# Where four operations run in a four-layer fp32 kernel: row sums, reciprocals, head order and the first squares

## The chip, the cores and the metric

One core of one Trainium2 chip. The metric is the device time of one execution in microseconds (us). Three runs of the kernel before gave 2515.85, 2521.76 and 2522.85 us; their median is 2521.76 us.

## The reference

The input is 256 tokens of width 2048, in float32. Four layers follow one another, each with an rmsnorm, an input projection, a mixer, an output projection and a residual:

- **E**: 16 heads of sliding-window attention with a sink, and 8 heads of a gated recurrence.
- **O**: 16 heads of stick-breaking attention.
- **D**: for each of 16 heads three softmaxes over dilated windows (dilations 1, 4, 16), mixed by their denominators, which is one softmax over all three sets of scores; times silu(z).
- **M**: 16 heads of causal softmax attention with a linear bias (with 256 tokens there is one block only); times silu(z).

The layers D and M take shift, scale and gate from `cond @ mod_w + mod_b`, with `cond = silu(c)` a single row of 2048; the scale enters as `norm_w * (1 + scale)`. A last rmsnorm ends it. Cut to what matters:

```
mod = silu(c) @ mod_w[i] + mod_b[i]          # one row of 3 x 2048 for each of D and M
h   = rms_norm(x, norm_w[i]) * (1 + scale) + shift
p   = softmax(q k^T * scale - slope * distance)   # masked
x   = x + gate * ((p v) * silu(z)) @ w_out
```

## The kernel before, in words

Weights come from HBM as **pieces** of 128 x 1024 float32 (512 KB), through `dma_ahead` (L221) on SP's queue into 6 `raw` buffers. ScalarE rounds a piece to `whi` (`split_hi`, L233, 6 buffers), VectorE takes the rest `wlo = raw - whi` (`split_lo`, L240, 4 buffers; L255), and TensorE multiplies hi by hi, lo by hi and hi by lo (`mm_step`, L1353). A raw buffer is free again when its `wlo` is made.

All engines are issued from one program written out by hand, in order (`tc.manual_schedule`). Work beside the matmuls is kept in Python generators. After each piece `pump` (L180) advances one evacuation (`ev`, `pri`) and the first three generators of the list `bg` by one `yield` (four in the last chunk of a layer's input projection). So a `yield` is a distance of one piece in the program, and each engine carries out its own instructions strictly in that order.

- `mod_unit` (L276) adds a piece of `mod_w` times silu(c) into `macc`, 128 x 512, on VectorE, 16 steps for each of 24 columns of 512: 8 of them in layer O, 12 in D, 4 in M. `mod_fin` (L288) then sums `macc` over the partitions on GpSimd (`partition_all_reduce`, L301), adds the bias row (L303) on GpSimd, for the scale also 1 and the norm's weight (L305, L306), and stores the row to HBM from GpSimd's queue (L309). It goes to the front of `bg`.
- `head_D` (L1066, two heads for each of 8 pairs) and `head_M` (L988, four heads for each of 4 groups) keep scores with the keys on partitions. The softmax's maximum and its sum are GpSimd's `partition_all_reduce` (`amax` L977, `asum` L978); VectorE subtracts, ScalarE takes Exp, VectorE takes the reciprocal of the sum (L1004, L1087), multiplies it by half of silu2(z), and TensorE multiplies by v. The four heads of M start in the same step as far as the list's width lets them.
- silu in E and O is made of Abs, Exp, Ln and Exp on ScalarE. In D and M `silu2_gen` (L342) takes Tanh. Line L1261 loads by name the set of ScalarE's functions that holds Exp and Ln.
- `Norm.rstd` (L397) takes the power -0.5 on GpSimd, and `hq` (L404) adds the shift of half a row on GpSimd at the start of D and M.
- In `layer_DM` (L962) a pair of D takes q and k of three windows (g = 0, 1, 2) and z; z's chunk stands ahead of q and k of g = 2.
- The first layer (L1312 to L1413) loads x in two halves of 128 tokens, `norm_x(b)` (L1322) squares a half on ScalarE with a sum, and `first_T` (L1331) transposes by a matmul with a diagonal that holds the norm. `norm_x(1)` stands between the second and the third `first_T` of the first half.

```
yield                       # mod_fin, L299 to L303
s = t2("msum")
G.partition_all_reduce(s, acc, channels=128, reduce_op=ReduceOp.add)
yield
G.tensor_tensor(r[0:1, :], r[0:1, :], s[0:1, :], op=ADD)
```

Of the kernel before, what the change touches and what calls it, by code (L numbers as in the profile page):

```python
# [18 lines left out]
D = 2048  # L19
# [85 lines left out]
def two_stacks_kernel(ctx: ExitStack, tc: tile.TileContext, A, out, layers="EODM"):  # L105
# [37 lines left out]
    def act(o, i, f, **k):  # L143
        S.activation(o, i, f, **k)  # L144

    def tt(o, a, b, op):
        V.tensor_tensor(o, a, b, op=op)  # L147
# [7 lines left out]
    def stt(o, a, s, b, op0, op1):  # L155
        V.scalar_tensor_tensor(o, a, s, b, op0=op0, op1=op1)  # L156
# [131 lines left out]
    def mod_fin(key):  # L288

        (i, p), col = key  # L290
        acc = mod_acc.pop(key)
        c0 = p * D + col * 512
        r = t2("mrow")
        G.dma_start(r[0:1, :], A["mod_b_2"][i, c0:c0 + 512].unsqueeze(0))
        nw = None
        if p == 1:
            nw = t2("mnw")
            G.dma_start(nw[0:1, :], A["norm_w_2"][i, col * 512:(col + 1) * 512].unsqueeze(0))
        yield  # L299
        s = t2("msum")  # L300
        G.partition_all_reduce(s, acc, channels=128, reduce_op=ReduceOp.add)  # L301
        yield
        G.tensor_tensor(r[0:1, :], r[0:1, :], s[0:1, :], op=ADD)  # L303
        if p == 1:
            G.tensor_scalar(r[0:1, :], r[0:1, :], 1.0, None, op0=ADD)  # L305
            G.tensor_tensor(r[0:1, :], r[0:1, :], nw[0:1, :], op=MUL)  # L306
        if col == 0:
            mod_row[i, p] = p_dr.tile([D], F32, name=f"mod{i}{p}")
        G.dma_start(mod_row[i, p][col * 512:(col + 1) * 512].unsqueeze(0), r[0:1, :])  # L309
# [652 lines left out]
    def layer_DM(which):  # L962
# [18 lines left out]
        def scores(s, hg, kT, qT, dm, sp):  # L981
# [3 lines left out]
            stt(s[:, 0:256], dm, -slope(hg), sp[:, 0:256], MUL, ADD)  # L985
            stt(s[:, 256:384], dm[:, 0:128], -slope(hg), sp[:, 256:384], MUL, ADD)

        def head_M(st, tri, h):  # L988
            hg = st["i"] * 4 + h
            qT, kT, v = tri["q"][0], tri["k"][0], tri["v"][0]  # L990
            s, m = t2("sM"), t2("mM")
            scores(s, hg, kT[:, h, :], qT[:, h, :], cl_h[0][:, 512:768], bank("s"))
            amax(m[:, 0:384], s[:, 0:384])
            yield
            yield
            tt(m[:, 128:256], m[:, 128:256], m[:, 256:384], MAX)
            tt(s[:, 0:256], s[:, 0:256], m[:, 0:256], SUB)
            tt(s[:, 256:384], s[:, 256:384], m[:, 128:256], SUB)
            act(s[:, 0:384], s[:, 0:384], AF.Exp)
            asum(m[:, 0:384], s[:, 0:384])  # L1000
            yield
            yield
            tt(m[:, 128:256], m[:, 128:256], m[:, 256:384], ADD)
            V.reciprocal(m[:, 0:256], m[:, 0:256])  # L1004
            while not st["z"]:
                yield
            stt(m[:, 0:256], m[:, 0:256], 0.5, st["z"][0][:, h, :], MUL, MUL)
            yield
            o = bank("oD")
            vh = lambda b: v[:, b, h * 128:(h + 1) * 128]  # L1010
            mm(o[:, 0:256], vh(0), s[:, 0:256], stop=False)
            mm(o[:, 128:256], vh(1), s[:, 256:384], start=False)
            tt(st["o"][:, h, :], o[:, 0:256], m[:, 0:256], MUL)
            finish(st)
            if not st:
                tri.clear()
# [49 lines left out]
        def head_D(st, pr, z):  # L1066
            h = pr["a"] * 2 + z
            s, l, m = pr.pop(("s", z)), pr.pop(("mx", z)), t2("mD")
            l, m = l[:, 0:256], m[:, 0:256]
            amax(m, l)  # L1070
            yield
            yield
            s1, s2 = s[:, 384:640], s[:, 640:896]
            tt(s[:, 0:256], s[:, 0:256], m, SUB)
            tt(s[:, 256:384], s[:, 256:384], m[:, 128:256], SUB)
            tt(nat(s1), nat(s1), by(m), SUB)
            tt(nat(s2), nat(s2), by(m), SUB)
            act(s[:, 0:896], s[:, 0:896], AF.Exp)
            yield
            yield  # L1080
            tt(by(l), by(s[:, 0:256]), nat(s1), ADD)
            tt(by(l), by(l), nat(s2), ADD)
            tt(l[:, 128:256], l[:, 128:256], s[:, 256:384], ADD)
            asum(m, l)
            yield
            yield
            V.reciprocal(m, m)  # L1087
            while pr["z"] is None:
                yield
            stt(m, m, 0.5, pr["z"][:, z * 256:(z + 1) * 256], MUL, MUL)  # L1090
            yield
            o = bank("oD")
            vh = lambda g, b: st["v"][g][0][:, b, h * 128:(h + 1) * 128]
            mm(o[:, 0:256], vh(0, 0), s[:, 0:256], stop=False)
            mm(o[:, 128:256], vh(0, 1), s[:, 256:384], start=False, stop=False)
            og = by(o[:, 0:256])
            for g in (1, 2):
                for b in range(2):
                    c0 = 128 + g * 256 + b * 128
                    mm(og[:, b, :], vh(g, b), s[:, c0:c0 + 128], start=False, stop=g == 2 and b == 1)  # L1100
            tt(st["o"][:, h, :], o[:, 0:256], m, MUL)
            pr["n"] += 1
            if pr["n"] == 2:
                pr.clear()
            finish(st)

        def qk_done(st, pr, g, half, ps):
            if half == 0:
                pr["qk"][g] = page("qk")
            reads(ev, fold(ps, pr["qk"][g], half, 128.0 ** -0.5 if half == 0 else 1.0))  # L1110
            if half == 1:
                pri.append(queue_D(st, pr, g))
# [12 lines left out]
        def z_done(pr, ps):  # L1125
            zr = t2("zr")
            reads(ev, fold(ps, zr, 0, 1.0))
            pri.append(z_gen(pr, zr))
# [7 lines left out]
        for i in range(4):  # L1136
            if NG == 1:
                st = {"z": [], "n": 0, "i": i}
                tri = {"q": [], "k": [], "v": []}
                b0 = i * 512  # L1140
                add512(ch, W, b0 + 2 * D, i == 0, lambda ps, tri=tri: reads(pri, ev_copy(ps, tri["v"])))
                add_w(ch, W, b0, "qT", lambda pg, tri=tri: keep_T(pg, tri["q"]), 128.0 ** -0.5)
                add_w(ch, W, b0 + D, "kT",
                      lambda pg, tri=tri, st=st: then(keep_T(pg, tri["k"]), lambda: start_M(st, tri)))
                add_w(ch, W, 3 * D + i * 512, "zr",
                      lambda pg, st=st: ev_silu2(pg, st["z"], lambda a: a.rearrange("p (h t) -> p h t", h=4)))
                continue
            st = {"v": [[], [], []], "n": 0, "i": i}
            for a in range(2):
                pr = {"a": a, "qk": [None] * 3, "z": None, "n": 0}  # L1150
                c0 = i * 512 + a * 256
                for g in range(3):
                    if a == 0:
                        add512(ch, W, (g * 3 + 2) * D + i * 512, i == 0 and g == 0,
                               lambda ps, st=st, g=g: reads(pri, ev_copy(ps, st["v"][g])))
                        ch[-1].dil = DIL[g]
                    if g == 2:
                        ch.append(Chunk(W, 9 * D + c0, 256, "w", done=lambda ps, pr=pr: z_done(pr, ps)))
                    for half in range(2):
                        ch.append(Chunk(W, (g * 3 + half) * D + c0, 256, "w",  # L1160
                                        done=lambda ps, st=st, pr=pr, g=g, half=half: qk_done(st, pr, g, half, ps)))
        return ch, setup

    dm_const = []
# [95 lines left out]
    with tc.manual_schedule():  # L1260
# [52 lines left out]
        load_x(0)  # L1313
        nc.sync.dma_start(cp[:, 0:128], A["const_p"][:, 0:128])
        nc.sync.dma_start(lnT, A["ln_first_t"])
        dma_ahead(2)
        load_x(1)
        dma_ahead(4)
        nc.sync.dma_start(cp[:, 128:C_W], A["const_p"][:, 128:C_W])
# [1 line left out]

        def norm_x(b):  # L1322

            for c0 in range(0, D, 512):
                norm.squares(b, c0, 512)
            norm.rstd(b)
            d = t2("diag")[:, 0:128]
            ts(d, ident, norm.r[b], None, MUL)
            return d
# [59 lines left out]
        for li, (l, ch, setup, oc, po) in enumerate(plans):  # L1389
# [6 lines left out]
            for ci, c in enumerate(ch):  # L1396
                if ci == len(ch) - 1:
                    width[0] = 4
                if c.bm:
# [2 lines left out]
                    hooks = {(0, 3): [(1, 0)], (1, 0): [(1, 1)], (1, 1): [(1, 2)], (1, 2): [(1, 3)]}  # L1402
                    if li == 0:
                        hooks = {(0, 0): [(0, 3)], (0, 1): [(1, 0)], (0, 2): [(1, 1)], (0, 3): [(1, 2)], (1, 0): [(1, 3)]}
                        ds = [dg0, None]
                        T = lambda b, q, ht: first_T(b, q, ht, ds[b])
                        for q in range(3):
                            T(0, q, ht)
                            split_hi(q + 1)
                            split_lo()  # L1410
                            if q == 1:
                                ds[1] = norm_x(1)
                        act(cr, cp[:, C_ONE:C_ONE + 256], AF.Copy)  # L1413
                    for b in range(2):
                        for j, p in enumerate(c.pieces):
# [115 lines left out]
```

## Time and profile before

| | before |
|---|---|
| median of three runs | 2521.76 us |
| the profiled execution | 2519.3 us |
| its span, first to last instruction | 2517.5 us |
| TensorE busy | 2445.0 us, 97% |
| VectorE busy | 1869.5 us, 74% |
| ScalarE busy | 1161.7 us, 46% |
| GpSimd busy | 372.4 us, 15% |
| TensorE's mean granted clock, as a share of full speed | 0.99 |

PE is TensorE's matmuls, PEld its weight loads, DVE VectorE, ACT ScalarE, POOL GpSimd, SP the queue that issues the large DMAs. "L255" is line 255 of the kernel. Behind an instruction the time that its engine stood idle just before it is given with what ended that idle time. "issue" as a releaser means that the engine waited for nothing that the profile shows. Busy shares are means over the span; a stall is read from its own stretch.

### The profile page before, as it was taken

To read this page: it belongs to the slowest core of one execution; us is meant where nothing else is said; L and a number is where in the kernel's file an instruction comes from. 1 tells how busy PE (TensorE), PEld (TensorE's weight loads), DVE (VectorE), ACT (ScalarE), POOL (GpSimd) and SP (SyncE) were. 2 spreads that over 40 slices of the span, in tenths; PEclk is the share of its full clock that TensorE was granted. 3 is DMA by queue.
4 is the path that set the end of the run, shared out by engine and by line. 5 is a ranking of instruction groups with operands and counts; after the bars stand their busy time and mean duration, and the time that the engine had idled before them with its cause. 6 is when DMAs were issued, how large, how long until landed. Compare 5 with 4: busy or idle time off the path is not lost.

```text
span 2517.5 us, 35660 instructions
## 1 busy us (share of the span) xinstructions
PE 2445.0 (97%) x13572; PEld 2128.7 (85%) x13572; DVE 1869.5 (74%) x2303; ACT 1161.7 (46%) x1459; POOL 372.4 (15%) x262
## 2 busy tenths in 40 slices
PE   7999999999999999999999999999999999998998
PEld 6888888988888888888788878888888888886887
DVE  5686976589999756678767776877687658786885
ACT  5556564545555644344344334444444443443443
POOL 1000110011311101011202121211012003222130
PEclk9999999999999999999999999999999999998999
DMA  7645445578888755777677767677776566775763
GB/s 218 192 127 175 135 143 179 166 258 286 275 291 278 232 177 179 237 238 236 205 246 229 229 208 243 218 251 236 245 229 207 184 197 212 230 227 167 250 207 120
DMA packets 408156, 538.90 MB, mean 214 GB/s; under 512 B 18784, under 2 KB 279040, under 8 KB 407984
## 3 DMA queue, kind: packets, MB, share of 16 engines
q1 hardware_dynamic: 403408, 527.97, 66.0%
q0 software_dynamic: 4576, 8.66, 1.3%
q8 instruction: 106, 1.74, 0.3%
q14 instruction: 66, 0.54, 0.1%
HBM read 534.41 MB, written 2.15 MB: 213 GB/s over the span
## 4 chain that ended last, share of the span: by engine, by line
PE 86%; issue 6%; DVE 4%; POOL 2%; ACT 1%; DMA 0%; POOLq 0%; ACTq 0%; DVEq 0%; SPq 0%
PE ps L138 80%; PE s L138 1%; DVE wlo L255 1%; PE oD L138 1%; PE lv L138 1%; DVE macc L156 1%; PE oO L138 0%; PE oA L138 0%; DVE mM L1004 0%; PE z L138 0%; ACT whi L144 0%; POOL msum L301 0%; PE X L138 0%; PE rc L138 0%; PE hT L138 0%
## 5 line engine op out<-in xcount | busy, mean ns | idle before, releaser
L255 DVE TENSOR_TENSOR wlo<-raw,whi 128x1024 fp32r<-128x1024 f32 x804 | 1031.6, 1286 | 439.1 <-PE ps L138 267.1
L144 ACT ACTIVATE whi<-raw 128x1024 fp32r<-128x1024 f32 x804 | 848.4, 1059 | 1051.5 <-PE ps L138 781.0
L138 PE MATMUL ps<-h,whi 128*128 128x512 f32 x3584 | 1134.5, 398 | 0.0
L138 PEld LDWEIGHTS ps<-h,wlo 128*128 128x128 f32 x3584 | 676.0, 189 | 172.6 <-DVE wlo L255 13.4
L138 PE MATMUL ps<-h,wlo 128*128 128x256 f32 x3584 | 708.7, 279 | 11.7 <-DVE wlo L255 11.7
L138 PE MATMUL ps<-whi,h 128*128 128x512 f32 (+1 forms) x2048 | 603.3, 374 | 1.5 <-DVE h L429 1.2
L138 PEld LDWEIGHTS ps<-h,whi 128*128 128x128 f32 x3584 | 549.5, 190 | 1.1
L138 PEld LDWEIGHTS ps<-whi,h 128*128 128x128 f32 x2048 | 379.5, 193 | 65.5 <-DVE h L429 3.3
L138 PE MATMUL ps<-wlo,h 128*128 128x512 f32 (+1 forms) x1024 | 379.8, 371 | 17.3 <-DVE wlo L255 17.3
L138 PE MATMUL ps<-whi,y 128*128 128x512 f32 (+1 forms) x1280 | 335.5, 349 | 3.9 <-DVE y L466 1.8
L156 DVE SCALAR_TENSOR_TENSOR macc<-raw,cs,macc 128x512 f32<-128x512 f32 x360 | 295.3, 820 | 0.6
L138 PEld LDWEIGHTS ps<-whi,y 128*128 128x128 f32 x1280 | 224.9, 189 | 34.9 <-DVE y L466 2.3
L138 PEld LDWEIGHTS ps<-wlo,h 128*128 128x128 f32 x1024 | 197.3, 193 | 48.1 <-DVE wlo L255 18.6
L138 PE MATMUL ps<-wlo,y 128*128 128x512 f32 (+1 forms) x640 | 222.0, 347 | 0.0
L301 POOL PARTITION_ALL_REDUCE msum<-macc x24 | 79.7, 3321 | 692.9 <-DVE macc L156 600.0
L138 PEld LDWEIGHTS ps<-wlo,y 128*128 128x128 f32 x640 | 121.3, 189 | 14.7
L303 POOL TENSOR_TENSOR mrow<-mrow,msum 1x512 f32<-1x512 f32 x24 | 39.4, 1642 | 189.9 <-issue 189.9
L977 POOL PARTITION_ALL_REDUCE mM<-sM x16 | 31.1, 1975 | 206.3 <-DVE sM L156 114.4
L977 POOL PARTITION_ALL_REDUCE mD<-mx x16 | 21.9, 1377 | 204.0 <-DVE mx L147 192.2
L401 POOL TENSOR_TENSOR rstd<-rstd,mh 128x1 f32<-128x1 f32 x10 | 5.7, 570 | 310.0 <-DVE rstd L153 310.0
L978 POOL PARTITION_ALL_REDUCE mM<-sM x16 | 44.8, 2835 | 26.9 <-ACT sM L144 21.0
L978 POOL PARTITION_ALL_REDUCE mD<-mx x16 | 34.7, 2173 | 93.4 <-DVE mx L147 80.4
(223 smaller groups left out, 1549.4 us busy)
## 6 DMA issues: line engine op xcount, KB each, us to landing
raw<-in_a_w_in_dram SPq DMA_DIRECT2D x320, 512.0 KB, 4.6
raw<-in_mod_w_dram SPq DMA_DIRECT2D x192, 512.0 KB, 4.7
raw<-in_w_in_odd_dram SPq DMA_DIRECT2D x128, 512.0 KB, 5.0
raw<-in_b_w_in_dram SPq DMA_DIRECT2D x128, 512.0 KB, 4.1
raw<-in_w_in_even_dram SPq DMA_DIRECT2D x100, 512.0 KB, 3.8
raw<-in_w_out_even_dram SPq DMA_DIRECT2D x32, 512.0 KB, 3.7
raw<-in_w_out_odd_dram SPq DMA_DIRECT2D x32, 512.0 KB, 4.5
raw<-in_a_w_out_dram SPq DMA_DIRECT2D x32, 512.0 KB, 4.5
```

What stands on the lines that cost most here:

```text
L138: PE.matmul(o, l, r, start=start, stop=stop, skip_group_check=True, **k)
L144: S.activation(o, i, f, **k)
L156: V.scalar_tensor_tensor(o, a, s, b, op0=op0, op1=op1)
L255: V.tensor_sub(u.lo, u.raw.t[:, u.k0 * u.n:(u.k0 + u.nk) * u.n], u.hi.bitcast(F32))
L301: G.partition_all_reduce(s, acc, channels=128, reduce_op=ReduceOp.add)
L303: G.tensor_tensor(r[0:1, :], r[0:1, :], s[0:1, :], op=ADD)
L401: G.tensor_tensor(r[:, 1:2], r[:, 0:1], mh[:, 0:1], op=ALU.pow)
L977: amax = lambda o, i: G.partition_all_reduce(o, i, channels=128, reduce_op=ReduceOp.max)
L978: asum = lambda o, i: G.partition_all_reduce(o, i, channels=128, reduce_op=ReduceOp.add)
```

## The change

- In `mod_fin` the bias is added on VectorE, four steps after the sum over partitions instead of one; for the scale, 1 and the norm's weight come in one VectorE instruction instead of two GpSimd ones.
- The reciprocal of the softmax's sums in `head_M` and `head_D` is made on ScalarE, as Ln and then Exp of the negative, instead of VectorE's RECIPROCAL. A `yield` follows it.
- Behind `amax` and behind `asum` there are three steps instead of two. In `head_M` the second and fourth head begin one step later, the third two steps; in `head_D` the second head of a pair one step.
- For the last pair of D, z's chunk moves behind q and k of g = 2.
- In the first layer, the last 512 of a half's squares go to VectorE (a product and a sum), `norm_x(1)` moves ahead of all `first_T`, the first piece is split ahead of it, and SP issues one piece instead of two ahead of x's second half.

```
 def mod_fin: ...
+        yield
+        yield
+        yield
-        G.tensor_tensor(r[0:1, :], r[0:1, :], s[0:1, :], op=ADD)
+        tt(r[0:1, :], r[0:1, :], s[0:1, :], ADD)
         if p == 1:
-            G.tensor_scalar(r[0:1, :], r[0:1, :], 1.0, None, op0=ADD)
-            G.tensor_tensor(r[0:1, :], r[0:1, :], nw[0:1, :], op=MUL)
+            stt(r[0:1, :], r[0:1, :], 1.0, nw[0:1, :], ADD, MUL)
...
+        def inverse(l):
+            act(l, l, AF.Ln)
+            act(l, l, AF.Exp, scale=-1.0)
 def head_M: ...
+            if h:
+                yield
+                if h == 2:
+                    yield
             amax(m[:, 0:384], s[:, 0:384])
+            yield
             yield
             yield
...
             asum(m[:, 0:384], s[:, 0:384])
             yield
             yield
+            yield
             tt(m[:, 128:256], m[:, 128:256], m[:, 256:384], ADD)
-            V.reciprocal(m[:, 0:256], m[:, 0:256])
+            inverse(m[:, 0:256])
+            yield
 def head_D: ...
+            if z:
+                yield
             amax(m, l)
+            yield
             yield
             yield
...
             asum(m, l)
             yield
             yield
-            V.reciprocal(m, m)
+            yield
+            inverse(m)
+            yield
...
+                    zc = Chunk(W, 9 * D + c0, 256, "w", done=lambda ps, pr=pr: z_done(pr, ps))
+                    if g == 2 and (i, a) != (3, 1):
+                        ch.append(zc)
...
+                if (i, a) == (3, 1):
+                    ch.append(zc)
...
-        dma_ahead(2)
+        dma_ahead(1)
         load_x(1)
 def norm_x: ...
-            for c0 in range(0, D, 512):
+            for c0 in range(0, D - 512, 512):
                 norm.squares(b, c0, 512)
+            sq = t2("sq")
+            tt(sq, x[:, b, D - 512:D], x[:, b, D - 512:D], MUL)
+            V.tensor_reduce(norm.ss[:, b * 8 + 7:b * 8 + 8], sq, axis=AX.X, op=ADD)
             norm.rstd(b)
...
-                        ds = [dg0, None]
+                        split_hi(1)
+                        split_lo()
+                        ds = [dg0, norm_x(1)]
                         for q in range(3):
                             T(0, q, ht)
-                            split_hi(q + 1)
+                            split_hi(q + 2)
                             split_lo()
-                            if q == 1:
-                                ds[1] = norm_x(1)
```

## Rows read from the trace of the kernel before

**Rows 1.** The page's first part: busy time of each engine, its share of the span, instructions.

```profile
PE 2445.0 (97%) x13572; PEld 2128.7 (85%) x13572; DVE 1869.5 (74%) x2303; ACT 1161.7 (46%) x1459; POOL 372.4 (15%) x262
```

**Rows 2.** Busy time by stretches of 50 us, in the view of windows: the stretch, then PE, PEld, DVE, ACT and POOL busy us (instructions), the granted clock of TensorE, the DMA engines' share, GB/s. Two stretches of layer O, one of D, three of M.

```profile
550.00:600.00 50.00, 49.05 (x256) 41.87 (x255) 48.14 (x63) 29.82 (x40) 14.05 (x10) 1.00 0.79 263
650.00:700.00 50.00, 49.68 (x259) 42.49 (x258) 49.41 (x63) 28.49 (x37) 10.94 (x8) 1.00 0.81 263
...
1200.00:1250.00 50.00, 45.00 (x230) 38.41 (x230) 39.00 (x52) 18.63 (x21) 13.26 (x9) 0.93 0.55 179
...
2100.00:2150.00 50.00, 46.80 (x241) 39.64 (x240) 48.23 (x59) 20.59 (x24) 18.82 (x8) 1.00 0.66 210
...
2200.00:2250.00 50.00, 47.28 (x234) 39.77 (x233) 45.50 (x51) 20.73 (x24) 20.10 (x10) 0.97 0.60 186
...
2300.00:2350.00 50.00, 38.58 (x177) 32.04 (x176) 36.06 (x44) 15.97 (x19) 18.02 (x9) 0.86 0.52 166
```

**Rows 3.** What TensorE waited for over the whole span: us in total, times, the longest.

```profile
PE ps L138 <- DVE wlo L255: 29.0, 7, 11.4
...
PE hT L138 <- DVE h L156: 3.6, 1, 3.6
```

**Rows 4.** GpSimd's instructions in order of time around the longest stall, in layer M: start, us, what, and in brackets the idle time before it and its releaser.

```profile
2291.09 3.38 POOL L977 PARTITION_ALL_REDUCE mM<-sM  x2 [47.32 <-PE s L138]
2294.38 3.80 POOL L301 PARTITION_ALL_REDUCE msum<-macc  x1
2305.25 1.28 POOL L303 TENSOR_TENSOR mrow<-mrow,msum 1x512 f32<-1x512 f32 x1 [7.08 <-issue]
...
2313.40 5.04 POOL L978 PARTITION_ALL_REDUCE mM<-sM  x2 [5.87 <-issue]
```

**Rows 5.** VectorE's instructions in the same stretch.

```profile
2301.10 1.22 DVE L255 TENSOR_TENSOR wlo<-raw,whi 128x1024 fp32r<-128x1024 f32 x1
2315.97 1.78 DVE L147 TENSOR_TENSOR mM<-mM 128x128 f32<-128x128 f32 x1 [13.65 <-POOL mM L978]
...
2321.39 1.16 DVE L255 TENSOR_TENSOR wlo<-raw,whi 128x1024 fp32r<-128x1024 f32 x1
```

**Rows 6.** GpSimd's instructions in groups over the whole span: count, busy us, mean ns of one, idle time before them and its releasers.

```profile
L301 POOL PARTITION_ALL_REDUCE msum<-macc x24 | 79.7, 3321 | 692.9 <-DVE macc L156 600.0 <-ACT whi L144 73.4 <-PE ps L138 19.4
L978 POOL PARTITION_ALL_REDUCE mM<-sM x16 | 44.8, 2835 | 26.9 <-ACT sM L144 21.0 <-issue 5.9
L303 POOL TENSOR_TENSOR mrow<-mrow,msum 1x512 f32<-1x512 f32 x24 | 39.4, 1642 | 189.9 <-issue 189.9
```

**Rows 7.** GpSimd in layer D: a DMA that it issues, and the sum over partitions that follows.

```profile
1361.08 0.48 POOL L298 DMA_DIRECT2D mnw<-in_norm_w_dram  x1
1362.60 4.05 POOL L301 PARTITION_ALL_REDUCE msum<-macc  x1 [1.04 <-DVE macc L156]
```

**Rows 8.** The chain that ended last, in order of time: start, us, what, number of instructions. The first four are the same stretch of the four groups of D, the last three are the same stretch of three groups of M.

```profile
1013.22 44.83 PE ps L138 x224
...
1255.83 44.83 PE ps L138 x224
...
1501.10 44.83 PE ps L138 x224
...
1736.55 44.83 PE ps L138 x224
...
2146.42 44.59 PE ps L138 x256
...
2245.00 44.59 PE ps L138 x256
...
2353.42 44.58 PE ps L138 x256
```

**Rows 9.** VectorE's instructions in groups over the whole span: the two reciprocals, and a sum of two operands of 512 a partition.

```profile
L1004 DVE RECIPROCAL mM<-mM 128x256 f32<-128x256 f32 x16 | 28.1, 1753 | 0.6
L1087 DVE RECIPROCAL mD<-mD 128x256 f32<-128x256 f32 x16 | 27.9, 1743 | 17.9 <-POOL mD L978 17.9
...
L147 DVE TENSOR_TENSOR E<-E,bq 128x512 f32<-128x512 f32 x16 | 11.0, 686 | 0.0
```

**Rows 10.** ScalarE's instructions in groups: one of 256 elements a partition.

```profile
L144 ACT ACTIVATE s<-Y 128x256 f32<-128x256 f32 x8 | 2.9, 378 | 10.6 <-PE Y L138 10.6
```

**Rows 11.** ScalarE in order of time at the first Tanh of layer D.

```profile
1089.65 1.06 ACT L144 ACTIVATE whi<-raw 128x1024 fp32r<-128x1024 f32 x1 [1.72 <-PE ps L138]
1090.73 1.28 ACT L144 ACT_TABLE_LOAD   x1
1092.03 0.63 ACT L144 ACTIVATE zs<-zr 128x512 f32<-128x512 f32 x1
```

**Rows 12.** All engines in order of time in the first 25 us.

```profile
9.16 6.23 PE L138 MATMUL hT<-diag,x 128*128 128x128 f32 x32 [9.16 <-DVE diag L151]
...
15.15 0.36 PE L138 MATMUL ps<-whi,h 128*128 128x256 f32 x1
...
18.84 1.57 DVE L151 TENSOR_SCALAR diag<-cp,rstd 128x128 f32<-128x128 f32 x1 [0.68 <-POOL rstd L401]
...
20.46 1.57 PE L138 MATMUL hT<-diag,x 128*128 128x128 f32 x8 [3.64 <-DVE h L156]
```

More of the change, by code (lines that the diff above doesn't have):

```diff
@@ L1156, in layer_DM @@
                         ch[-1].dil = DIL[g]
-                    if g == 2:
-                        ch.append(Chunk(W, 9 * D + c0, 256, "w", done=lambda ps, pr=pr: z_done(pr, ps)))
+                    zc = Chunk(W, 9 * D + c0, 256, "w", done=lambda ps, pr=pr: z_done(pr, ps))
+                    if g == 2 and (i, a) != (3, 1):
+                        ch.append(zc)
                     for half in range(2):
```

## The prediction

> **What bounds the kernel now.** I read the page's busy line first, then the busy time in stretches of 50 us, then TensorE's waits, then the engines around single stalls, and at the end the chain. TensorE is busy 97% of the span [rows 1], so only its 72.5 us of idle time, and the slower clock that follows a long stall, are to be had. In the stretches [rows 2] that idle time is gathered: 0.95 and 0.32 us in layer O, but 5.0 in a stretch of D, and 3.2, 2.7 and 11.4 us in three of M. TensorE's largest wait is for wlo from VectorE: 29.0 us in 7 waits, one of 11.4 [rows 3].
>
> Why is wlo late, when VectorE is no more than 74% busy? GpSimd's order around the 11.4 us tells it [rows 4]: a bias add stands 7.08 us without a releaser before it starts, and the next sum for a head 5.87 us. Each time GpSimd passes from a sum over partitions to ordinary arithmetic, or back, such a gap comes. VectorE, in order, waits 13.65 us for that sum, with wlo behind it: the last wlo ends at 2302.3, the next begins at 2321.4 [rows 5]. Of this gap of 19.1 us, 11.4 reach TensorE; the pieces split ahead cover 7.7. All 24 bias adds have the gap, 189.9 us in all [rows 6]. A DMA issued by GpSimd brings none: a sum begins 1.04 us after one, and that wait is for its data [rows 7]. So without arithmetic between the sums D and M should lose both gaps.
>
> What the stalls cost, clock included, comes from the chain [rows 8]. The four groups of D have the same work; their marks lie 242.6, 245.3 and 235.5 us apart. The last distance has no stall, so D loses 7.2 + 9.8 = 17.0. In M the marks lie 98.6 and 108.4 apart, and the stretches hold 2.7 and 11.4 us of idle time [rows 2]: 8.7 us more of it made 9.8 us more, 1.13 for one, the clock's part included. M's 3.2 + 2.7 + 11.4 = 17.3 us so cost 19.5. Together **36.5 us**.
>
> **The change part by part.**
>
> *Bias adds and the waits.* With GpSimd free of them, the 36.5 us are the upper end. The lower end is a third, 12: sums still queue behind each other (3.3 us for a column, 2.8 for a head of M [rows 6]), a stall of three sums at once is no code gap, and the store of a row now waits on GpSimd for VectorE's add, with the next sum behind it. Against that queue stand the third step behind each sum and the staggered heads: a step is a piece, 2.79 us, about one sum. I give back a tenth: **-33.0**. A stall that goes leaves ScalarE's wait for a raw piece next, which is late only because wlo freed its buffer late.
>
> *VectorE's balance.* Off: 32 reciprocals, 28.1 + 27.9 = 56.0 us [rows 9]. On: 24 adds and 8 combined instructions. A one-partition instruction is not in the trace; bounded by 0 and by the full tile's 0.69 us, taken at the latter because length along the row is the same, 32 x 0.69 = 22. Net -34 in D and M, where VectorE has room. In O nothing comes off: 8 adds and 4 more, 8.3 us, where VectorE is busy 48.1 and 49.4 of 50 [rows 2]. Between 0 (its idle time elsewhere takes them) and 8.3 I take **+1.5**, since TensorE hardly waits there yet.
>
> *The reciprocal on ScalarE.* Two activations of 256, 0.38 us each [rows 10]. But the first Tanh of D costs a table load of 1.28 us, from the end of one activation to the start of the next 1.32 [rows 11]; that set then serves Tanh and Exp. No row shows a Ln after it. Loads per inverse lie between 0 and 2 (one for Ln, one for Exp). I take 2: the set that holds both is loaded by name in L1261, and the load before Tanh shows that a function outside the loaded set brings its own. An inverse then holds ScalarE 2 x 1.32 + 2 x 0.38 = 3.4 us; all 32 make 109 us on an engine that is half idle. A pair of D is 6.8, under the 7.7 of cover. In M four inverses in four steps (11.2 us) make 13.6, with four whi at 1.06 17.8: 6.6 behind, under 7.7 as well. If the cover is thinner, 8 pairs and 4 groups pay; bounds 0 and 1.5 each, I take 0.5: **+6.0**. The Ln also waits for GpSimd with whi queued behind it on ScalarE, three steps after the sum; priced with these bounds.
>
> The Trainium skill speaks against this edit: ScalarE: Activation LUTs, section "What ACT_TABLE_LOAD costs", puts every switch at 1.28 us for the load and 1.38 for a drain, 2.66 in all. The load agrees with the row; the drain does not show there, the Tanh starting 0.02 us behind the load. By the page an inverse would hold ScalarE 6.1 us and a pair 12.2, and the sum would be that of rival D.
>
> *The start.* TensorE's first transposes cover 9.16 to 15.4 (the first piece starts at 15.15), then it stands 3.64 us at 20.46, because the second half's diagonal is made at 18.84 to 20.41 [rows 12]; the wait is the one of 3.6 us for h [rows 3]. With `norm_x(1)` ahead of the transposes that diagonal is ready before they end. Bounds: the 3.64 and as much again for the slow clock after it, 7.3, against +2 if x's second half holds up ScalarE and VectorE in front of the first h. The transposes themselves take until 15.4, so some lateness is free. SP's second piece moves behind two DMAs of x and is late by about those; it is needed only after the first. Two squares on VectorE replace ScalarE's, beside the transposes. I take **-4.5**.
>
> *The rest.* Longer heads: a head of M may take about 12 steps of the 32 pieces of its group, so nothing waits. At the end of D the last pair takes four steps more, and z's move starts it one chunk, four pieces, earlier: 0, bounds -2 and +2. A sum that lasts three steps longer in the list holds one of three places from the heads: 0 for the same reason.
>
> Sum: 2519.3 - 33.0 + 1.5 + 6.0 - 4.5 = **2489.3**, against the profiled execution's own time (span 2517.5 and 1.8 around it). That execution lies 2.5 us under the median of the runs, 2521.8, and within their spread.
>
> **The rivals.**
>
> *A, the hold of ScalarE eats half* (0.16). ScalarE's queue puts Ln behind a late sum or Exp, and whi behind it; DVE's multiplication waits for it where z is ready. For it: 64 loads that were not there. Against: ScalarE idles mostly because it waits for TensorE to free whi. Twelve groups at 2.0 instead of 0.5: +18, 2507; with a weaker gain at the sums up to 2514.
>
> *B, GpSimd stays late* (0.08). The sums' own queue, not the gaps, sets the waits, and only a third comes back: 2519.3 - 12 + 1.5 + 6 - 4.5 = 2510. Against it: the same sums stand in all four groups of D, and the third has no stall [rows 8].
>
> *C, the gaps stay* (0.06). Something else on GpSimd, the power of the norm or the shift, keeps bringing them. For it: both stay there. Against: they stand only at a layer's edge. Then the start's gain and the new costs are left: 2519.3 + 1.5 + 6 - 4.5 = 2522.
>
> *D, slower* (0.08). A switch costs ScalarE about double the row. An inverse is then 2 x 2.64 + 0.76 = 6.0, a pair 12.1, 4.4 over the cover; four heads of M 24.2 and 4.2 for whi against 11.2 of time, 9.5 over. 8 x 4.4 + 4 x 9.5 = 73: 2519.3 - 33 + 1.5 - 4.5 + 73 = 2556. It decides against the change where the twelve groups lose over 36 us, 3 each beyond the cover: a switch of about 2.1 us. Against it: the row's 1.32.
>
> **How the numbers follow.** The forecast has 0.62 with a range of its own of 2474 to 2505. With A and B inside, 2474 to 2512 leaves out D, C and the tails, 2 in 10. About 0.3%, 7.6 us, can be told from no change: faster is under 2514.2, slower over 2529.4. Faster: 0.62, 0.13 of A, 0.07 of B, 0.01 of C, 0.83. Slower: D, 0.08. The same: 0.09.
>
> **What would show it.** GpSimd's 5.9 and 7 us without releaser gone inside D and M; VectorE's waits on L977 and L978 near 0; marks of D about 236 us apart, of M 95; 60 or more table loads of 1.28 us; TensorE's idle time at 20 us gone. Wrong would be: waits of PE for wlo behind a whi that stands behind Ln, new stalls in O, or gaps that stay.

## The result, and the profile after

After takes **2476.61 us** (median of 4 runs, 2475.38 to 2477.78), before 2520.11 in the runs beside it (2515.85 to 2522.85). The ratio is 0.9829, 95% interval 0.9812 to 0.9846: 43.5 us, 1.7%. The profiled execution's span is 2475.7, against 2517.5.

The page's first part (compare [rows 1]): TensorE stands idle 2475.7 - 2434.7 = 41.0 us instead of 72.5. GpSimd loses 67.5 us of work, ScalarE gains 103.4.

```profile
PE 2434.7 (98%) x13572; PEld 2121.6 (86%) x13572; DVE 1820.6 (74%) x2307; ACT 1265.1 (51%) x1583; POOL 304.9 (12%) x222
```

Stretches of [rows 2] in after (PE, PEld, DVE, ACT, POOL busy, granted clock, DMA share, GB/s): all but full, the clock at 1.00.

```profile
550.00:600.00 50.00, 50.00 (x263) 42.96 (x262) 47.63 (x64) 28.89 (x37) 6.12 (x4) 1.00 0.83 274
...
1200.00:1250.00 50.00, 50.00 (x262) 43.02 (x261) 39.80 (x54) 28.08 (x31) 9.46 (x5) 1.00 0.76 238
...
2200.00:2250.00 50.00, 49.73 (x276) 42.57 (x275) 42.23 (x53) 31.73 (x36) 7.92 (x4) 1.00 0.82 263
2300.00:2350.00 50.00, 50.00 (x287) 43.60 (x286) 37.22 (x41) 28.56 (x32) 9.82 (x5) 1.00 0.77 243
```

TensorE's waits in after, against [rows 3]: the 29.0 us for wlo are 0.2. The three others shown are one of 2.1 us for h at the start and two for y at the end of layer D.

```profile
PE ps L138 <- DVE h L156: 2.1, 1, 2.1
PE ps L138 <- ACT y L144: 2.1, 1, 2.1
PE ps L138 <- DVE y L468: 0.5, 1, 0.5
PE ps L138 <- DVE wlo L255: 0.2, 1, 0.2
```

GpSimd in after, in order of time, at the third group of M, where [rows 4] had two gaps: a column's sum, a maximum, two heads' sums, then the store. Every wait has an owner, the longest 2.71 us.

```profile
2265.94 3.31 POOL L301 PARTITION_ALL_REDUCE msum<-macc  x1
2269.15 1.50 POOL L979 PARTITION_ALL_REDUCE mM<-sM  x1
2273.37 2.80 POOL L980 PARTITION_ALL_REDUCE mM<-sM  x1 [2.71 <-ACT sM L144]
...
2280.23 0.50 POOL L311 DMA_DIRECT2D mod<-mrow  x1 [0.59 <-DVE mrow L147]
```

VectorE in the same stretch, against [rows 5]: wlo comes every 2 to 4 us, and the bias add stands among them at 2279.26.

```profile
2266.76 2.57 DVE L255 TENSOR_TENSOR wlo<-raw,whi 128x1024 fp32r<-128x1024 f32 x1
...
2269.86 1.27 DVE L255 TENSOR_TENSOR wlo<-raw,whi 128x1024 fp32r<-128x1024 f32 x1
...
2279.26 0.67 DVE L147 TENSOR_TENSOR mrow<-mrow,msum 1x512 f32<-1x512 f32 x1
```

The chain of after, in order of time. The first four are the marks of D from [rows 8], then one mark at the start of M's input projection (in before at 2027.65) and three equal stretches of M, 94.8 and 94.0 us apart.

```profile
1005.79 44.83 PE ps L138 x224
...
1241.25 44.83 PE ps L138 x224
...
1476.69 44.83 PE ps L138 x224
...
1712.14 44.82 PE ps L138 x224
...
2007.41 65.92 PE ps L138 x410
2133.84 33.44 PE ps L138 x192
2228.66 33.44 PE ps L138 x192
2322.64 33.44 PE ps L138 x192
```

D's marks lie 235.46, 235.44 and 235.45 us apart: all three are now the distance that had no stall. Differences between the marks of the two chains split the 41.8 us of span:

| stretch | before to after | predicted |
|---|---|---|
| start, up to the mark of layer E (51.41, now 47.56) and of layer O (481.91, now 478.27) | -3.6 | -4.5 |
| layer O, to 882.24, now 876.31 | -2.3 | +1.5 |
| from there to the first mark of D | -1.5 | - |
| D, first mark to last | -17.0 | part of -33.0 |
| last mark of D to the mark of M, 291.10, now 295.27 | +4.2 | 0 |
| M, from its mark to the end | -21.6 | part of -33.0 |
| the reciprocal on ScalarE, in no one stretch | see below | +6.0 |

The -1.5 can't be put down to the change: this stretch took 129.5 or 131.0 us in every kernel below, 129.48 in after and 131.02 in the kernel of experiment 10, which is the same as after up to there. Where it took 131.0, TensorE's granted clock dips in it (0.72 in before from 958 to 964 us, 0.81 in 10 from 946 to 955); in after it stays at 1.00.

### The profile page after: what moved, and what is told of

It reads as the page before. It is cut to its first block, busy times and chain, and to the rows that moved or that the text cites. A ratio compares the mean times of both kernels' runs of the same rounds, so it can differ in the third digit from the quotient of the medians.

```text
span 2475.7 us, 35664 instructions
## 1 busy us (share of the span) xinstructions
PE 2434.7 (98%) x13572; PEld 2121.6 (86%) x13572; DVE 1820.6 (74%) x2307; ACT 1265.1 (51%) x1583; POOL 304.9 (12%) x222
## 4 chain that ended last, share of the span: by engine, by line
PE 92%; issue 4%; DVE 1%; POOL 1%; ACT 0%; DMA 0%; SPq 0%; POOLq 0%; ACTq 0%; DVEq 0%
PE ps L138 86%; PE s L138 1%; PE oD L138 1%; PE lv L138 1%; DVE wlo L255 0%; PE z L138 0%; PE oO L138 0%; PE oA L138 0%; PE rc L138 0%; DMA x<-in_x_dram 0%; PE X L138 0%; PE hT L141 0%; PE oB L138 0%; DVE h L431 0%; POOL rstd L403 0%
## 5 line engine op out<-in xcount | busy, mean ns | idle before, releaser
L156 DVE SCALAR_TENSOR_TENSOR macc<-raw,cs,macc 128x512 f32<-128x512 f32 x360 | 286.7, 796 | 0.6
L301 POOL PARTITION_ALL_REDUCE msum<-macc x24 | 81.8, 3409 | 671.7 <-DVE macc L156 670.4
L144 ACT ACT_TABLE_LOAD x65 | 83.4, 1283 | 5.2 <-DVE mM L147 4.1
L156 DVE SCALAR_TENSOR_TENSOR sD<-cld,s 128x256 f32<-128x256 f32 x64 | 23.2, 383 | 33.7 <-PE s L138 33.5
```

## The experiments

Times are medians; ratios are to before, with their 95% interval. Each edit is made on after unless it says before.

**1. The adds back on GpSimd**, their four steps kept.

```
 yield x4
-tt(r[0:1, :], r[0:1, :], s[0:1, :], ADD)            # VectorE
+G.tensor_tensor(r[0:1, :], r[0:1, :], s[0:1, :], op=ADD)
 ...                                                  # 1 and the norm's weight likewise
```

> The changed kernel with the bias adds (and the 1 and the weight) back on GpSimd, all else as changed, the four steps behind the sum included. Theory (the gaps on GpSimd between a sum over partitions and arithmetic made the stalls): each add has its 7 to 8 us gap again, and stalls return where a gap falls among a head's sums; about half to nearly all of the 17.0 us of D and of M's 19.5 come back, 2495 to 2513 us. Rival (the extra steps behind each sum and the staggered heads hide the sums, gap or no gap): 2476 to 2484 us, and the marks of D stay 235.5 us apart.

2477.5 us, 0.9836 (0.9822 to 0.9851): 0.9 above after. All 24 gaps are back: in GpSimd's groups the add has `190.9 <-issue 190.9`. TensorE waits 2.5 us for wlo in three waits, and D's marks lie 235.46, 237.16 and 235.44 us apart. So the theory that the gaps must go falls here, and the rival's range holds. GpSimd in this kernel, at a pair of D:

```profile
1347.44 4.05 POOL L301 PARTITION_ALL_REDUCE msum<-macc  x1 [1.04 <-DVE macc L156]
1351.39 1.35 POOL L980 PARTITION_ALL_REDUCE mD<-mx  x1
1360.78 1.32 POOL L306 TENSOR_TENSOR mrow<-mrow,msum 1x512 f32<-1x512 f32 x1 [8.04 <-issue]
...
1375.41 3.61 POOL L981 PARTITION_ALL_REDUCE mD<-mx  x2 [8.46 <-issue]
```

Both gaps stand there, but behind the pair's maxima and ahead of its sums, where GpSimd has time.

**2. Only the adds, on before**: on VectorE, four steps after the sum; heads, reciprocal and start as in before.

```
 def mod_fin: ...                                     # on before
+yield x3
-G.tensor_tensor(r[0:1, :], r[0:1, :], s[0:1, :], op=ADD)
+tt(r[0:1, :], r[0:1, :], s[0:1, :], ADD)
```

> The kernel before with nothing but the adds moved to VectorE, four steps behind the sum. Theory (gaps): D's 17.0 us come back whole, the marks 235.5 us apart; in M the 11.4 us stall goes, the two of 3.2 and 2.7 us, behind three sums and three reciprocals in a row, stay; 2519 - 17 - 13 = 2487 to 2492 us. Rival (steps or reciprocals did it): 2510 to 2522 us.

2486.37, 0.9871 (0.9855 to 0.9888): in kind as expected, 0.6 below the range. D's marks are 235.46 apart, so all of D's 17.0 come back. In M two waits for wlo are left, 3.20 and 2.73 us, and there GpSimd has no gap: it makes the sums of three heads at once (8.62 us for three), and VectorE three RECIPROCALs of 1.75 us in a row. From its mark, in the chain of this kernel, to the end of the span at 2484.7 us M takes 475.6 us; before takes 489.9 and after 468.3.

```profile
2009.12 65.93 PE ps L138 x410
```

**3. RECIPROCAL back on VectorE.**

```
-inverse(m)
+V.reciprocal(m, m)                                   # head_M likewise
```

> The changed kernel with RECIPROCAL on VectorE in place of Ln and Exp, the step behind it kept. Theory (the reciprocal's place costs and gives nothing once the heads are staggered, since 3.4 us on ScalarE and 1.75 us on VectorE both lie under the cover): 2474 to 2480 us, one table load in place of 65. Rival (taking the 56 us off VectorE is what freed M): 2482 to 2490 us, with waits of TensorE for wlo in M. Second rival (the table loads cost 6 us, as the prediction has it): about 2470 us.

2477.09, 0.9833 (0.9818 to 0.9848). The interval takes in after: the place of the reciprocal makes no difference that can be measured.

**4. Without the added steps** of `head_D` and `head_M`.

```
-            if h:
-                yield
-                if h == 2:
-                    yield
 ...                                                  # and the third step behind amax and asum,
 ...                                                  # the one behind inverse, head_D's if z
```

> The changed kernel without the added steps in the heads: no later entry, two steps behind each sum, none behind the inverse. Theory (gaps are the main cause; the steps hide the sums of three heads that stand in a row): D's marks stay 235.5 us apart within 1 us, M loses 3 to 8 us; 2479 to 2487 us. Rival (the steps did the work): 2495 us or more, with VectorE waiting for GpSimd at L979 and L980 by 30 us or more in all.

2485.33, 0.9864 (0.985 to 0.9879): 8.7 above after, inside the range. D is whole (marks 235.45 to 235.47 apart). The 8.7 are two things: M takes 482.1 us from its mark, 13.9 longer than in after, more than the 3 to 8 that I had expected, and D's end is 4.9 shorter (see 10). M has two waits for whi, 4.00 and 3.55 us: three heads in lockstep bring three inverses in one block of 10 us on ScalarE, and whi stands behind it. ScalarE, the last inverse of such a block:

```profile
2091.73 1.28 ACT L144 ACT_TABLE_LOAD   x1
2093.03 0.42 ACT L144 ACTIVATE mM<-mM 128x256 f32<-128x256 f32 x1
2093.46 1.28 ACT L144 ACT_TABLE_LOAD   x1
2094.76 0.42 ACT L144 ACTIVATE mM<-mM 128x256 f32<-128x256 f32 x1
2095.08 1.99 ACT L144 ACTIVATE whi<-raw 128x1024 fp32r<-128x1024 f32 x2
```

**5. The inverse made twice over**, four loads and four activations for each: Ln and Exp, and once more with the opposite sign.

```
 def inverse(l):
     act(l, l, AF.Ln)
     act(l, l, AF.Exp, scale=-1.0)
+    act(l, l, AF.Ln)
+    act(l, l, AF.Exp, scale=1.0)
```

> The changed kernel with each inverse done twice over on ScalarE (Ln, Exp, Ln, Exp; the value stays 1/x): 129 table loads, an inverse holds ScalarE 6.8 us instead of 3.4. If ScalarE's hold is all under cover, as the run with RECIPROCAL suggests: under 2480 us. By the prediction's rival D (cover 7.7 us): a pair 13.6, 5.9 over; a group of M 27 and 4 against 11 of time, 12 over: 8 x 5.9 + 4 x 12 = 95, 2570 us. With a cover twice that, as whi is two pieces further ahead than wlo: 2480 to 2510 us, TensorE waiting for whi from ScalarE.

2514.15, 0.9972 (0.9961 to 0.9982): 37.5 above after, outside all three ranges, nearest to 2480 to 2510. Windows of D and of M, first of this kernel, then of after:

```profile
1000.00:1900.00 900.00, 900.00 (x4898) 779.40 (x4897) 656.72 (x820) 471.50 (x510) 107.42 (x73) 1.00 0.72 236
2010.00:2450.00 440.00, 417.17 (x2193) 353.18 (x2192) 297.60 (x367) 278.24 (x318) 101.22 (x53) 0.98 0.64 207
```

```profile
1000.00:1900.00 900.00, 900.00 (x4898) 779.42 (x4897) 657.47 (x819) 426.17 (x455) 107.53 (x73) 1.00 0.74 235
2010.00:2450.00 440.00, 439.73 (x2407) 380.49 (x2406) 326.18 (x390) 242.97 (x280) 101.76 (x54) 1.00 0.69 220
```

D pays nothing: 900.00 of 900 us busy, although a pair now holds ScalarE 4 x 3.4 = 13.6 us: two whi stand between a pair's two inverses (at 1374.61 and 1376.03 us in the second group). M pays all of it: four heads hold it 8 x 3.4 = 27 us in a group, and TensorE idles 23 us more, at a granted clock of 0.98 instead of 1.00. So ScalarE held twice as long would have hurt, but by 37 and in M alone, not by the 95 that rival D's sum gives for this load.

**6. z's chunk in its old place** in the last pair of D.

```
-if g == 2 and (i, a) != (3, 1):
+if g == 2:
     ch.append(zc)
```

> The changed kernel with z's chunk of the last pair of D back in its old place. Theory (the added steps make the last pair late, and z's move gives back four steps of it): the stall at D's end grows from 2.6 us by about four steps of flushing without matmuls, 5 to 11 us: 2481 to 2488 us. Rival (the end of D is set by z or by the norm, not by the last pair): 2474 to 2478 us.

2477.38, 0.983 (0.9813 to 0.9846). The wait for y at D's end grows from 2.1 to 2.6 us, and no more. I had expected 2481 to 2488: a miss; from D's last mark to M's it is 295.71 us instead of 295.27, so the move is worth about 0.4. **After once more**, on the chip of experiments 10 and 11, the two that its text means:

> The changed kernel itself, on the same chip as the two that follow, so that a difference of 2 to 5 us can be read: 2475 to 2478 us.

2476.17, 0.9829 (0.9814 to 0.9844).

**7. Late adds alone, on before**: three more steps ahead of the adds, which stay on GpSimd.

```
 def mod_fin: ...                                     # on before
+yield x3
 G.tensor_tensor(r[0:1, :], r[0:1, :], s[0:1, :], op=ADD)
```

> The kernel before with three more steps between a column's sum and its add, the add still on GpSimd: the gap of 7 to 8 us stays but stands in the queue behind the sums that heads ask for meanwhile. Theory 1 (what hurts is a gap that stands ahead of a head's sum in GpSimd's order): D's marks near 236 us, M's 11.4 us stall gone or moved; 2488 to 2500 us. Theory 2 (the time a head leaves for its sum decides, so the steps inside the heads are needed while gaps stay): 2508 to 2520 us, stalls at other places.

2502.96, 0.9929 (0.9914 to 0.9944): 17 us, between the two expected ranges. M's 11.4 us stall is gone (0.5 and 1.7 are left in its place), the two short ones stay. One of D's two long distances is left (244.76 us), with a stall of 6.21. GpSimd and then VectorE around it:

```profile
1363.68 2.61 POOL L981 PARTITION_ALL_REDUCE mD<-mx  x1 [6.27 <-DVE mx L147]
1372.95 1.28 POOL L306 TENSOR_TENSOR mrow<-mrow,msum 1x512 f32<-1x512 f32 x1 [6.66 <-issue]
...
1383.97 1.81 POOL L981 PARTITION_ALL_REDUCE mD<-mx  x1 [5.77 <-issue]
```

```profile
1385.81 1.75 DVE L1090 RECIPROCAL mD<-mD 128x256 f32<-128x256 f32 x1 [12.55 <-POOL mD L981]
```

The adds now fall between the sums of the pair's two heads, and the second sum gets both gaps.

**8. The head steps alone, on before**: those of 4 but the one behind the inverse.

```
 def head_M, head_D: ...                              # on before
+yield                                                # head starts, behind amax, behind asum
```

> The kernel before with nothing but the added steps in the heads (third step behind each sum, later entry); adds on GpSimd one step behind the sum, reciprocals on VectorE. Theory 1 (a gap ahead of a head's sum hurts): a gap of 7.8, an add and a gap of 5.9 make 16 us against one more step of 2.8, so D keeps 8 us or more of its 17, the whole 2495 to 2510 us. Theory 2 (the steps give enough cover): 2481 to 2490 us, D's marks 235.5 us apart.

2516.34 (10 runs), 0.9986 (0.9977 to 0.9995): about 4 us, less than either theory expected. The stalls only move. Here the second head's maximum comes a step later and so behind the adds, and VectorE waits 10.98 us for it; TensorE then stands 6.79 us. GpSimd there:

```profile
1366.06 1.40 POOL L303 TENSOR_TENSOR mrow<-mrow,msum 1x512 f32<-1x512 f32 x1 [8.89 <-issue]
...
1377.47 1.08 POOL L977 PARTITION_ALL_REDUCE mD<-mx  x1 [6.03 <-issue]
```

**9. The adds and the reciprocal both back**, steps kept. Late adds gave 17 us, head steps 4, the start 4 to 5: 25 or 26. But the kernel of 1 gained 42 with its gaps. Either the two kinds of steps work together, or Ln on ScalarE takes a wait that would hold up wlo on VectorE.

```
 ...                                                  # the edits of 1 and of 3 together
```

> After's kernel with the adds back on GpSimd (four steps after the sum) and RECIPROCAL on VectorE in place of Ln and Exp; head steps, start and z's place as in after. Two theories of why the adds cost nothing on GpSimd in the kernel with Ln and Exp, although late adds alone gave 17 us and head steps alone 4. (1) Interplay: late adds and head steps together give every sum its distance, whichever engine waits for it: 2475 to 2484 us, all 24 gaps of about 8 us still there, no wait of TensorE over 2 us in D, marks of D 235.5 to 237.5 us apart. (2) The place of the wait: Ln on ScalarE takes the wait for a late sum, so that VectorE and wlo don't stand behind it; with RECIPROCAL on VectorE the waits come back: 2486 to 2500 us, VectorE waiting 5 us or more for L980 or L981 and TensorE for wlo in D or M, marks of D over 240 us apart at least once.

2478.65, 0.9839 (0.9823 to 0.9856): the steps work together. The gaps are there (191.9 us), D's marks are 235.46, 236.32 and 235.45 apart, and TensorE's waits for wlo are 1.9 us in all. GpSimd and then VectorE at the same pair:

```profile
1361.24 1.34 POOL L306 TENSOR_TENSOR mrow<-mrow,msum 1x512 f32<-1x512 f32 x1 [8.56 <-issue]
...
1375.86 3.60 POOL L981 PARTITION_ALL_REDUCE mD<-mx  x2 [8.97 <-issue]
```

```profile
1369.14 1.22 DVE L255 TENSOR_TENSOR wlo<-raw,whi 128x1024 fp32r<-128x1024 f32 x1
...
1377.70 1.75 DVE L1105 RECIPROCAL mD<-mD 128x256 f32<-128x256 f32 x1 [6.67 <-POOL mD L981]
1379.37 1.16 DVE L255 TENSOR_TENSOR wlo<-raw,whi 128x1024 fp32r<-128x1024 f32 x1
```

VectorE does wait, 6.67 us, and 9.0 us pass between two wlo (1370.36 to 1379.37); TensorE stands only 0.57 us behind them. In 7 and in 8 the same distance was 15.6 us (1372.92 to 1388.47) and 16.5 (1364.27 to 1380.73), and TensorE stood 6.2 and 6.8. So the pieces split ahead cover 8 to 10 us here, and the sum of this kernel comes late by hardly more than that.

**10. The last pair of D short**: no added steps and RECIPROCAL there, all else as in after.

```
+last = st["i"] == 3 and pr["a"] == 1
-if z:
+if z and not last:
     yield
 ...                                                  # likewise behind amax, asum and the inverse
```

> The changed kernel, but the last pair of D goes without the added steps and with RECIPROCAL. Theory (the added steps make the output projection wait at D's end, where no next pair covers them: 295.3 us from the last mark of D to M in the changed kernel, 290.4 without any added step): 4 to 5 us less than the changed kernel, 2470 to 2474 us, no wait for y at D's end. Rival (that stretch differs by the clock alone): 2475 to 2478 us.

**2471.88**, 0.9811 (0.9794 to 0.9827), the lowest median of all. There is no wait for y, and from D's last mark to M's it is 290.27 us instead of 295.27. The steps do it, not the RECIPROCAL that came with the edit: 3 has RECIPROCAL and the steps, and 295.27 as well. With RECIPROCAL for every other head too:

> As the one before, and RECIPROCAL on VectorE for every head: neither table loads nor inverses. Theory (both places lie under the cover): within 2 us of the one before, 2469 to 2474 us. Rival (the inverse is what keeps M free of stalls): 2476 us or more.

2472.5, 0.9814 (0.98 to 0.9829): no difference from that, as in 3.

## Why the prediction was right, and where it was not

**The gaps and the stalls (-33.0).** Right in place and kind; measured -17.0 in D and -21.6 in M, -38.6 in all. In D the marks gave the size to a tenth. I had kept a tenth back for sums that queue up; nothing was kept. In M 19.5 was foreseen in full and 21.6 came. Experiment 2 splits it: the 11.4 us stall cost 14.3 (489.9 against 475.6), where 1.13 for one makes 12.9, and the two short ones cost 7.3 (475.6 against 468.3), not 6.7. The 1.13 was too low because both distances that it was read from had a stall; without one the distance is 94.0, so the stall of 2.7 us cost 4.6. Experiment 2 shows that the adds' move alone does D and M's longest stall; the 3.2 and 2.7 of M, which I had put under the same cause, were three heads in lockstep (2 and 4), and the head steps took them, with either reciprocal (3).

**"Without arithmetic between the sums D and M should lose both gaps."** True, but as a reason it was too narrow. That the gaps go is sufficient (2), not necessary (1, 9). What costs is where a gap stands: the adds with a gap on each side make a block of 15 to 23 us in GpSimd's queue, and it hurts when a sum that VectorE soon needs is issued behind it. The change has two remedies, no block, or a block between maxima and sums with three steps to spare; for D and M's longest stall either does, to within 2 us (2; 1 and 9). Whether the add on VectorE would do as well one step behind the sum, without the three added ones, was not run. Late adds without the head steps (7) and head steps without late adds (8) each put a sum behind the block again.

**VectorE's balance (+1.5 in O).** The add of one row took what I had taken from the full tile. The groups of after:

```profile
L147 DVE TENSOR_TENSOR mrow<-mrow,msum 1x512 f32<-1x512 f32 x24 | 16.1, 672 | 0.0
L144 ACT ACT_TABLE_LOAD x65 | 83.4, 1283 | 5.2 <-DVE mM L147 4.1
```

But O went 2.3 us faster, not slower: 398.04 us against 400.33. With the adds late but on GpSimd it is 398.50 (1), 398.70 (9) and 399.24 (7), and in 8, whose layer O is that of before, about 399.4. The same layer O differs by 0.7 and 0.9 us there, so what part lateness and what part the engine has is open. The sign was wrong, the size small.

**The reciprocal on ScalarE (+6.0).** The hold was right: two loads for each inverse (64 of the 65), 1.28 + 0.42 twice, 3.4 us. Its price was not: 3 puts it at nothing, since the cover that I had named held everywhere. It held because of the head steps: without them M loses 13.9 us with Ln and Exp (4), but 7.3 with RECIPROCAL (2). Rival A's wait exists, VectorE waits 29.0 us for whi ahead of wlo where before had 7.4, but TensorE's 0.2 us show that it is covered. Rival D needed 2.1 us a switch; the rows of 4 show 1.30 from a load's start to the next activation's. The Trainium skill (ScalarE: Activation LUTs, section "What ACT_TABLE_LOAD costs") adds a drain of 1.38 us to each load. The load agrees, 1283 ns over 65; the drain shows in none of the rows here, where an activation begins 0.02 us behind its load, and the next load 0.01 behind the activation.

**The start (-4.5).** Right: -3.6 in this trace, about -5 over all. TensorE's first transposes begin at 8.71 instead of 9.16, but here the second half's diagonal is made only at 14.89 to 16.46, because x's second half comes late, and a wait of 2.13 us remains. In after, in order of time:

```profile
14.89 1.57 DVE L151 TENSOR_SCALAR diag<-cp,rstd 128x128 f32<-128x128 f32 x1 [0.68 <-POOL rstd L403]
16.54 0.50 PE L138 MATMUL ps<-whi,h 128*128 128x256 f32 x2 [2.13 <-DVE h L156]
```

That wait belongs to this execution. In the second trace of after the diagonal is made at 13.70 to 15.27 and the wait is gone, and the other kernels with this start wait at most 1.1 us for h there. Up to the mark of layer O nothing else of the change is at work. It lies at 481.2 to 482.6 us in the three chains with the old start (before, 2, 7), and at 475.7 to 478.3 in nine with the new one, of which after's is the latest; the means, 481.9 and 476.9, are 5.0 apart.

**The rest (0, bounds -2 and +2).** This is the term that cost time: +4.2 at D's end, outside its bounds. I let z's move pay for four more steps of the last pair. It does not (6), because no piece of work follows that could cover those steps: the output projection waits for that pair's y. TensorE, in before and then in after:

```profile
1953.23 0.74 PE L138 MATMUL ps<-whi,y 128*128 128x512 f32 x2 [1.83 <-DVE y L466]
```

```profile
1928.62 0.50 PE L138 MATMUL ps<-whi,y 128*128 128x512 f32 x1 [2.09 <-ACT y L144]
1929.88 0.77 PE L138 MATMUL ps<-whi,y 128*128 128x512 f32 x2 [0.53 <-DVE y L468]
```

Experiment 10 takes the steps out there and gets 5.0 back. The wait itself is only 0.8 longer (2.09 + 0.53 against 1.83); the rest of the 4.2 is mostly the clock. Windows as in [rows 2], behind the wait and just ahead of the mark of M, in before and then in after:

```profile
1953.00:1957.00 4.00, 3.77 (x16) 3.12 (x17) 1.40 (x2) 1.06 (x1) 0.00 (x0) 1.00 0.48 148
2019.60:2024.00 4.40, 4.40 (x39) 4.40 (x39) 2.44 (x4) 2.01 (x4) 2.75 (x2) 1.00 0.00 0
```

```profile
1930.00:1934.00 4.00, 4.00 (x11) 3.15 (x12) 0.33 (x1) 0.00 (x0) 0.00 (x0) 0.57 0.19 70
1998.00:2003.00 5.00, 5.00 (x32) 5.00 (x31) 1.56 (x3) 1.29 (x3) 2.56 (x2) 0.66 0.00 0
```

Behind the longer wait TensorE's clock falls towards the lower of its two levels, 0.57 in the mean, while it stays at 1.00 in before: matmul by matmul this costs 1.6 us. The dip ahead of M's mark costs 1.5 more; the kernel of 10 has such a dip too, so whether the change brings it is not shown.

In this trace the terms missed by -5.6, -3.8, about -6, +0.9 and +4.2, and the change of layer by -1.5: together -11.8, the distance from 2489.3 to 2477.5, the profiled execution of after by the same reckoning (its span and 1.8). 2489 was too high mainly because the bounds for covered work were each paid in part. The measured time lies only 2.6 us above the lower end of the range, 2474, and part of that is luck: without the loss at D's end, as in 10, it would have come out below.

## What to carry to other kernels

A slow switch on a side engine costs by its place in that engine's queue: look which result stands behind it and how many steps it has, and either take the switch out or put it where nothing is due. Steps added to a pipeline are free while later work covers them; at the end of a layer, where none follows, leave them out. Two edits that give 17 and 4 us alone may do nearly all of it together, so their gains must not be added up from single runs.

## What the runs showed of the hardware

A wlo on VectorE that begins beside GpSimd's sum of a column ends just behind that sum. In D and M of after (1000 to 2450 us) 385 wlo had no GpSimd instruction beside them, and none took over 1.23 us. 16 began while GpSimd summed a column (L301, 3.2 us or more): one in the last us of its sum, which took 1.21, and 15 earlier, which took 2.46 to 3.26, and each of these ended 0.07 to 0.09 us behind the sum. The 2.57 us at 2266.76 above is one: the sum beside it ends at 2269.25, wlo at 2269.33. In before all 13 that began so ended 0.07 to 0.09 us behind it as well. No run took the two apart, so why is not shown; it stayed covered here.
